# PEER gate spreading: the one-hot factors written by VectorE and ScalarE alone, in a two-block transformer kernel

## The chip, the core and the metric

The kernel runs on one core of a Trainium2 chip. The metric is the time of one execution on the device in microseconds (us). The engines are named as in the profile: PE (TensorE matmuls), PEld (its weight loads), DVE (VectorE), ACT (ScalarE), POOL (GpSimd) and SP (SyncE, which issues most DMAs). All engines run their own instruction lists in order and meet at semaphores.

## The reference, cut to what matters

Two transformer blocks run over 512 tokens of width 1024. The first block ends in a PEER layer: each token picks, in each of 8 heads, 16 experts out of 128 x 128, each with a softmax gate. Its heart is

```
v1, i1 = lax.top_k(s1, PEER_TOPK)
v2, i2 = lax.top_k(s2, PEER_TOPK)
...
e1 = jnp.take_along_axis(i1, ci // PEER_TOPK, axis=-1)
e2 = jnp.take_along_axis(i2, ci % PEER_TOPK, axis=-1)
idx = e1 * N_KEYS + e2
gates = jax.nn.softmax(sc, axis=-1).astype(h.dtype)
...
u = peer_u[ix]
a = jax.nn.gelu(jnp.einsum('td,thkd->thk', hx, u), approximate=False)
vsel = peer_v[ix]
return jnp.einsum('thk,thkd->td', gx * a, vsel)
```

The second block (Hyena, neighbourhood attention, pooling, and a mixture of 16 experts) is not touched by the change.

## The kernel before

For the last 128 of the 512 tokens the kernel gathers the chosen rows of `peer_u` and `peer_v`. For the first 384 (three tiles of 128 tokens) it computes all 16384 experts densely and weights them with a dense matrix of gates, which is zero for experts that were not chosen. That matrix is built by `spread` and is what the change touches.

A token has 128 chosen (e1, e2, gate) triples, one on each partition after a transpose: the tiles `e1T`, `e2T` and `gT` hold, per partition (one of the 128 choices) and token, the first index, the second index and the gate. The token's 128 x 128 gate matrix is then one matmul, contracted over the 128 choices, of a one-hot of e2 with a one-hot of e1 that carries the gate. `spread(t, step)` does 8 blocks of 16 tokens for each of 3 token tiles, so 24 blocks; each block has two halves (`hb`) of 8 tokens. `iob` is a constant with the values 0 to 127, each repeated 8 times. Per half:

- L572, DVE: `ob` = (iob == e1), 128 x 1024, in bf16, written densely with the 8 tokens innermost.
- L574, POOL: `of` = ob times gT, fp32, written with the token as the outer index, so that neighbouring writes lie 512 bytes apart.
- L578, DVE: `ob2` = (iob == e2), bf16, dense. In the rows it stands as `ob` or `ob_` with a number, with `e2T` as its input.
- L579, ACT: `oq` = copy of ob2 to fp32, also written with neighbours 512 bytes apart.
- L583, PE: 8 matmuls `gps` <- of, oq; the trace counts 16, since it shows each fp32 matmul as two.
- L585, ACT: two evacuations of `gps` into `st`; after both halves SP stores the block to `Gd` (L587).

After each block `step` runs two things. `early_u(1)` computes one of 40 expert groups ahead: it loads `uraw`, splits it into `uhi` (L400, ACT) and `ulo` (L401: POOL for every third group, otherwise DVE), does 24 matmuls into `aps` (L85 to L87), and ACT writes `gle` (L595). And it advances `decode`, the top-16 selection of the next token tile, mostly small DVE instructions, with four table loads and four 128 x 2048 copies (L532) on ACT in the stage.

A scheduler orders this part of the program on each engine. After it the list is written by hand (L715 on): the dense expert matmuls, paced gathers, then the second block. The pools `of`, `oq`, `ob`, `gps` and `aps` have two buffers each.

Of the kernel before, what the change touches and what calls it, by code (L numbers as in the profile page):

```python
# [9 lines left out]
F32 = mybir.dt.float32  # L10
F32R = mybir.dt.float32r
BF16 = mybir.dt.bfloat16
I32 = mybir.dt.int32
U32 = mybir.dt.uint32
AF = mybir.ActivationFunctionType
ALU = mybir.AluOpType
# [4 lines left out]
P = 128  # L21
# [343 lines left out]
def peer(px, tc, I, E):  # L365
    nc = tc.nc
    mm = nc.tensor.matmul
    act = nc.scalar.activation
    vtt = nc.vector.tensor_tensor
    vts = nc.vector.tensor_scalar  # L370
    stt = nc.vector.scalar_tensor_tensor
    ptt = nc.gpsimd.tensor_tensor
# [11 lines left out]
    e1T = kp.tile([P, TD], BF16, name="e1T", tag="e1T")  # L384
    e2T = kp.tile([P, TD], BF16, name="e2T", tag="e2T")
    gT = kp.tile([P, TD], F32, name="gT", tag="gT")
# [5 lines left out]
    EARLY = [e for e in range(P) if e % 16 in AHEAD]  # L392
    Ad = drp.tile([len(EARLY), P, TD], F32, name="Ad")

    def u_split(e, lo_engine):
        raw = up.tile([P, KD, P], F32, name="uraw", tag="uraw", bufs=4)
        nc.sync.dma_start(raw, I["peer_uT"][e])
        hi = up.tile([P, KD, P], F32R, name="uhi", tag="uhi")
        lo = up.tile([P, KD, P], F32R, name="ulo", tag="ulo")
        act(hi, raw, AF.Copy)  # L400
        lo_engine.tensor_tensor(lo, raw, hi.bitcast(F32), op=ALU.subtract)  # L401
        return hi, lo

    def u_matmuls(hi, lo):
        ps = papp.tile([P, TD], F32, name="aps", tag="aps")
        for k in range(KD):
            mm3(ps, hi[:, k], lo[:, k], hh[:, k, :TD], hl[:, k, :TD], k == 0, k == KD - 1)
        return ps

    with ExitStack() as qx:  # L410
        gp = qx.enter_context(tc.tile_pool(name="gp", bufs=2))
# [3 lines left out]
        iob = gp.tile([P, P, 8], BF16, name="iob", tag="iob", bufs=1)  # L415
# [150 lines left out]
        def spread(t, step):  # L566
            for blk in range(8 * t, 8 * t + 8):
                st = gp.tile([P, P, 16], F32, name="st", tag="st")
                for hb in range(2):
                    c0 = 16 * blk + 8 * hb  # L570
                    ob = gp.tile([P, P, 8], BF16, name="ob", tag="ob")
                    vtt(ob, iob, e1T[:, None, c0:c0 + 8].to_broadcast([P, P, 8]), op=ALU.is_equal)  # L572
                    of = gp.tile([P, 8, P], F32, name="of", tag="of")
                    ptt(of.rearrange("p t e -> p e t"), ob,  # L574
                        gT[:, None, c0:c0 + 8].to_broadcast([P, P, 8]), op=ALU.mult)
                    oq = gp.tile([P, 8, P], F32, name="oq", tag="oq")
                    ob2 = gp.tile([P, P, 8], BF16, name="ob2", tag="ob2")
                    vtt(ob2, iob, e2T[:, None, c0:c0 + 8].to_broadcast([P, P, 8]), op=ALU.is_equal)  # L578
                    act(oq.rearrange("p t e -> p e t"), ob2, AF.Copy)  # L579
                    for t4 in range(2):  # L580
                        ps = pp.tile([P, 4, P], F32, name="gps", tag="gps")
                        for j in range(4):
                            mm(ps[:, j], oq[:, 4 * t4 + j], of[:, 4 * t4 + j], start=True, stop=True)  # L583
                        o = 8 * hb + 4 * t4
                        act(st[:, :, o:o + 4], ps.rearrange("p t e -> p e t"), AF.Copy)  # L585
                for c in range(2):
                    nc.sync.dma_start(Gd[c][:, blk], st[:, 64 * c:64 * c + 64])  # L587
                step()
# [3 lines left out]
        def early_u(count):  # L592
            for n in itertools.islice(early, count):
                gl = up.tile([P, TD], F32, name="gle", tag="gle", bufs=2)
                act(gl, u_matmuls(*u_split(EARLY[n], nc.gpsimd if n % 3 == 0 else nc.vector)), AF.Gelu)  # L595
                nc.sync.dma_start(Ad[n], gl)

        for h in range(8):
# [1 line left out]
        for _ in decode(0):  # L600
            early_u(1)
        for t in range(NDT):
            dec = decode(t + 1)

            def step():
                early_u(1)
                for _ in itertools.islice(dec, 2):
                    pass

            spread(t, step)  # L610
            for _ in dec:
                pass

    early_u(len(EARLY))


# [887 lines left out]
```

## Time and profile before

| | us |
|---|---|
| median of 3 runs | 2873.01 (2872.85 to 2874.96) |
| the profiled execution | 2876.98 |
| its span, first to last instruction | 2875.2 |
| PE busy in the span | 2587.0 (90%) |
| DVE / ACT / POOL busy | 1482.8 / 941.4 / 718.8 |
| the stage of `spread` | 468.2 to about 694.5 |

The span is what the trace shows; the execution's own time is 1.8 us more. A busy share is an average over stages with different limits, so the stage of `spread` has to be read by itself.

### The profile page before, as it was taken

Reading aid. Unit: us, or ns where it says so; the run is one execution under the profiler, and the core shown is the slowest. Engines: PE = TensorE matmul, PEld = TensorE weight load, DVE = VectorE, ACT = ScalarE, POOL = GpSimd, SP = SyncE. Lnnn points to the kernel's source line nnn. Section 1 sums busy time; section 2 is a strip of 40 time slices with the busy share of each in tenths; the row PEclk is TensorE's granted clock in tenths of the full one; section 3 lists DMA queues with packets and bytes.
Section 4 is the critical chain, followed back from the end, with each engine's and each line's share of the span. In section 5 each row is a group of like instructions: output and inputs, shape, how many; then the busy total and the mean of one; then the engine's idle time right before and its main releaser. Section 6 shows DMA issues by size and latency. Waiting matters only on the chain.

```text
span 2875.2 us, 32379 instructions
## 1 busy us (share of the span) xinstructions
PE 2587.0 (90%) x12449; PEld 1806.2 (63%) x12449; DVE 1482.8 (52%) x2552; ACT 941.4 (33%) x1412; POOL 718.8 (25%) x427
## 2 busy tenths in 40 slices
PE   5798998799999999999999899969888888788887
PEld 4566888699888888888988777643322223222232
DVE  6853799984677777778878855330100101011011
ACT  5563437786333333333333434220000000000001
POOL 3411003565344444444435322110000000000000
PEclk9799999999999999999999999989999999999999
DMA  6622323467788988988889522289999999999997
GB/s 237 231 74 77 111 94 123 149 222 265 276 311 309 330 303 315 324 307 319 315 317 318 188 98 72 74 323 412 427 428 428 427 428 428 427 428 428 427 428 300
DMA packets 200451, 826.37 MB, mean 287 GB/s; under 512 B 16776, under 2 KB 85768, under 8 KB 172265
## 3 DMA queue, kind: packets, MB, share of 16 engines
q1 hardware_dynamic: 160088, 681.19, 60.4%
q0 software_dynamic: 38016, 138.43, 13.6%
q10 hardware_dynamic: 2192, 4.69, 0.5%
q8 instruction: 98, 1.61, 0.2%
q14 instruction: 57, 0.46, 0.0%
HBM read 787.02 MB, written 37.22 MB: 287 GB/s over the span
## 4 chain that ended last, share of the span: by engine, by line
PE 66%; DMA 19%; DVE 11%; ACT 2%; issue 1%; POOL 1%; ACTq 0%; SPq 0%; DVEq 0%; POOLq 0%
DMA wch<-in_w_up 10%; DMA wch<-in_w_gate 7%; PE acc L87 6%; PE acc L86 6%; PE acc L85 6%; PE aps L87 5%; PE aps L86 5%; PE aps L85 5%; PE y L1323 5%; PE upp L1298 4%; PE gp L1298 4%; PE mmp L85 4%; PE mmp L87 4%; PE mmp L86 4%; PE gps L583 2%
## 5 line engine op out<-in xcount | busy, mean ns | idle before, releaser
L1305 DVE TENSOR_TENSOR sg<-sg,upp 128x512 f32<-128x512 f32 x32 | 22.0, 688 | 752.6 <-PE upp L1298 752.6
L87 PE MATMUL aps<-hh,ulo 128*128 128x384 f32 x1024 | 347.1, 339 | 9.4 <-DVE ulo L401 6.4
L85 PE MATMUL aps<-hh,uhi 128*128 128x384 f32 x1024 | 348.5, 340 | 2.8 <-ACT uhi L400 1.8
L86 PE MATMUL aps<-hl,uhi 128*128 128x384 f32 x1024 | 347.5, 339 | 0.0
L1298 PE MATMUL upp<-wch,XB 128*64 128x512 f32 x1024 | 271.0, 627 | 51.0 <-DMA wch<-in_w_up 51.0
L85 PE MATMUL acc<-vh,wh 128*128 128x512 f32 x768 | 300.0, 391 | 1.9 <-ACT wh L81 1.9
L87 PE MATMUL acc<-vh,wl 128*128 128x512 f32 x768 | 300.7, 392 | 0.0
L86 PE MATMUL acc<-vl,wh 128*128 128x512 f32 x768 | 299.9, 390 | 0.3 <-DVE vl L82 0.3
L1298 PE MATMUL gp<-wch,XB 128*64 128x512 f32 x1024 | 263.7, 612 | 31.3 <-DMA wch<-in_w_gate 31.1
L625 POOL DMA_INDIRECT row<-in_peer_u,gidx x128 | 203.8, 1592 | 260.2 <-DVE gscr L632 228.6
L625 POOL DMA_INDIRECT row<-in_peer_v,gidx x128 | 208.1, 1626 | 238.6 <-DVE gacc L638 210.8
L1323 PE MATMUL y<-wch,aT 128*64 128x512 f32 x1024 | 246.6, 597 | 11.9 <-ACT aT L1312 11.9
L1298 PEld LDWEIGHTS upp<-wch,XB 128*64 128x64 f32 x1024 | 84.6, 144 | 215.2 <-issue 143.5
L400 ACT ACTIVATE uhi<-uraw 128x1024 fp32r<-128x1024 f32 x128 | 135.6, 1059 | 220.6 <-DMA uraw<-in_peer_uT 168.1
L1298 PEld LDWEIGHTS gp<-wch,XB 128*64 128x64 f32 x1024 | 81.3, 141 | 200.3 <-issue 149.3
L87 PEld LDWEIGHTS aps<-hh,ulo 128*128 128x128 f32 x1024 | 194.7, 190 | 12.2 <-DVE ulo L401 8.4
L85 PEld LDWEIGHTS aps<-hh,uhi 128*128 128x128 f32 x1024 | 195.1, 191 | 6.8 <-ACT uhi L400 2.0
L86 PEld LDWEIGHTS aps<-hl,uhi 128*128 128x128 f32 x1024 | 194.7, 190 | 4.0
L401 DVE TENSOR_TENSOR ulo<-uraw,uhi 128x1024 fp32r<-128x1024 f32 x114 | 149.8, 1314 | 85.1 <-ACT uhi L400 84.8
L1304 ACT ACTIVATE sg<-gp 128x512 f32<-128x512 f32 x32 | 19.1, 597 | 482.9 <-PE gp L1298 482.9
L1323 PEld LDWEIGHTS y<-wch,aT 128*64 128x64 f32 x1024 | 77.2, 137 | 150.0 <-issue 130.5
L638 DVE SCALAR_TENSOR_TENSOR gacc<-row,ga,gacc 128x1024 f32<-128x1024 f32 x128 | 164.1, 1282 | 2.3
(406 smaller groups left out, 4560.9 us busy)
## 6 DMA issues: line engine op xcount, KB each, us to landing
wch<-in_w_gate SPq DMA_DIRECT2D x64, 2048.0 KB, 32.5
wch<-in_w_up SPq DMA_DIRECT2D x64, 2048.0 KB, 32.1
wch<-in_w_down SPq DMA_DIRECT2D x62, 2048.0 KB, 33.9
uraw<-in_peer_uT SPq DMA_DIRECT2D x128, 512.0 KB, 7.7
vraw<-in_peer_v SPq DMA_DIRECT2D x128, 512.0 KB, 7.0
Gd<-st SPq DMA_DIRECT2D x48, 512.0 KB, 4.1
gg<-Gd SPq DMA_DIRECT2D x16, 1536.0 KB, 17.6
wada<-in_w_ada SPq DMA_DIRECT2D x19, 1024.0 KB, 5.2
```

What stands on the lines that cost most here:

```text
L85: mm(out, lh, rh, start=first, stop=False)
L86: mm(out, lh, rl, start=False, stop=False)
L87: mm(out, ll, rh, start=False, stop=last)
L400: act(hi, raw, AF.Copy)
L401: lo_engine.tensor_tensor(lo, raw, hi.bitcast(F32), op=ALU.subtract)
L583: mm(ps[:, j], oq[:, 4 * t4 + j], of[:, 4 * t4 + j], start=True, stop=True)
L625: nc.gpsimd.indirect_dma_start(out=row, out_offset=None, in_=I[src], in_offset=bass.IndirectOffsetOnAxis(ap=gidx[:, j:j + 1], axis=0))
L638: stt(outp, row, ga[:, n - P:n - P + 1], outp, op0=ALU.mult, op1=ALU.add)
L1298: mm(ps[64 * e:64 * e + 64], xT[:, k, 64 * e:64 * e + 64], gu[w][e][:, o:o + T], start=k == 0, stop=k == KD - 1)
L1304: act(sg, ps2[0], AF.Silu)
L1305: vtt(sg, sg, ps2[1], op=ALU.mult)
L1323: mm(y[c][64 * e:64 * e + 64], aT[:, fb, 64 * e:64 * e + 64], dn[e][:, o:o + T], start=fc == 0 and fb == 0, stop=fc == 3 and fb == 3)
```

## The change

`of` is now the bare one-hot of e1, written by DVE directly as fp32 in the layout that POOL wrote before. The gate is multiplied in on the other side: instead of one ACT copy of 1024 elements there are 8 of 128, one for each token, each of which reads every eighth element of ob2 (16 bytes apart), writes densely, and has the token's gate as its per-partition scale. The split `ulo` of `early_u` always runs on DVE. No GpSimd tensor instruction is left in this stage.

```
-                    ob = gp.tile([P, P, 8], BF16, name="ob", tag="ob")
-                    vtt(ob, iob, e1T[:, None, c0:c0 + 8].to_broadcast([P, P, 8]), op=ALU.is_equal)
                     of = gp.tile([P, 8, P], F32, name="of", tag="of")
-                    ptt(of.rearrange("p t e -> p e t"), ob,
-                        gT[:, None, c0:c0 + 8].to_broadcast([P, P, 8]), op=ALU.mult)
-                    oq = gp.tile([P, 8, P], F32, name="oq", tag="oq")
+                    vtt(of.rearrange("p t e -> p e t"), iob, e1T[:, None, c0:c0 + 8].to_broadcast([P, P, 8]),
+                        op=ALU.is_equal)
                     ob2 = gp.tile([P, P, 8], BF16, name="ob2", tag="ob2")
                     vtt(ob2, iob, e2T[:, None, c0:c0 + 8].to_broadcast([P, P, 8]), op=ALU.is_equal)
-                    act(oq.rearrange("p t e -> p e t"), ob2, AF.Copy)
+                    oq = gp.tile([P, 8, P], F32, name="oq", tag="oq")
+                    for j in range(8):
+                        act(oq[:, j], ob2[:, :, j], AF.Copy, scale=gT[:, c0 + j:c0 + j + 1])
...
-                act(gl, u_matmuls(*u_split(EARLY[n], nc.gpsimd if n % 3 == 0 else nc.vector)), AF.Gelu)
+                act(gl, u_matmuls(*u_split(EARLY[n], nc.vector)), AF.Gelu)
```

Lines behind the edit move up by one: the new L572 writes `of`, L575 writes ob2, L578 is the scaled conversion, L584 the evacuation and L594 `gle`.

On ACT, one block of the third token tile stood like this before:

```order
L400 ACTIVATE uhi<-uraw 128x1024
L595 ACTIVATE gle<-aps 128x384
L585 ACTIVATE st<-gps 128x128x4 x2
L579 ACTIVATE oq<-ob_4833 128x128x8
L585 ACTIVATE st<-gps 128x128x4 x2
L579 ACTIVATE oq<-ob_4853 128x128x8
```

and one block of the second token tile stands like this now:

```order
L578 ACTIVATE oq<-ob_4308,gT 128x128 x3
L584 ACTIVATE st<-gps 128x128x4
L578 ACTIVATE oq<-ob_4308,gT 128x128 x5
L578 ACTIVATE oq<-ob_4333,gT 128x128 x7
L594 ACTIVATE gle<-aps 128x384
L578 ACTIVATE oq<-ob_4333,gT 128x128
L584 ACTIVATE st<-gps 128x128x4
L400 ACTIVATE uhi<-uraw 128x1024
L584 ACTIVATE st<-gps 128x128x4 x2
```

Two conversions became 16, and three of the four evacuations of a block stand behind both halves' conversions.

On DVE, two blocks without decode work stood like this before:

```order
L401 TENSOR_TENSOR ulo<-uraw,uhi 128x1024
L572 TENSOR_TENSOR ob<-iob,e1T 128x1024
L578 TENSOR_TENSOR ob_4679<-iob,e2T 128x1024
L572 TENSOR_TENSOR ob<-iob,e1T 128x1024
L578 TENSOR_TENSOR ob_4699<-iob,e2T 128x1024
L572 TENSOR_TENSOR ob<-iob,e1T 128x1024
L578 TENSOR_TENSOR ob_4756<-iob,e2T 128x1024
L572 TENSOR_TENSOR ob<-iob,e1T 128x1024
L578 TENSOR_TENSOR ob_4776<-iob,e2T 128x1024
```

and one such block stands like this now:

```order
L401 TENSOR_TENSOR ulo<-uraw,uhi 128x1024
L572 TENSOR_TENSOR of<-iob,e1T 128x128x8
L575 TENSOR_TENSOR ob_4308<-iob,e2T 128x1024
L575 TENSOR_TENSOR ob_4333<-iob,e2T 128x1024
L572 TENSOR_TENSOR of<-iob,e1T 128x128x8
```

The number of one-hot instructions is the same; `of` takes the place of `ob` with another output, and `ulo` now comes once in every block.

## Rows read from the trace of the kernel before

**Rows 1.** Busy time of each engine, granted PE clock and DMA, by stretches of the stage.
```profile
core 0: us, PE busy (x) PEld busy (x) DVE busy (x) ACT busy (x) POOL busy (x), PEclk, DMA share, GB/s
468.00:500.00 32.00, 26.55 (x162) 25.67 (x162) 29.94 (x40) 22.96 (x25) 23.38 (x9) 0.88 0.39 134
530.00:560.00 30.00, 18.69 (x114) 17.38 (x114) 30.00 (x106) 20.18 (x26) 13.23 (x5) 0.89 0.37 131
...
620.00:660.00 40.00, 39.82 (x282) 38.82 (x281) 30.76 (x25) 36.55 (x42) 28.01 (x12) 1.00 0.62 221
...
468.00:695.00 227.00, 197.44 (x1331) 190.28 (x1331) 192.84 (x312) 187.12 (x207) 140.41 (x56) 0.95 0.52 186
```

**Rows 2.** Groups of instructions from 468 to 695 us: busy us, mean ns, idle before.
```profile
L572 DVE TENSOR_TENSOR ob<-iob,e1T 128x1024 bf16<-128x1024 bf16 x48 | 67.1, 1397 | 23.5 <-POOL of L574 23.5
L578 DVE TENSOR_TENSOR ob<-iob,e2T 128x1024 bf16<-128x1024 bf16 x48 | 42.9, 893 | 0.0
L401 DVE TENSOR_TENSOR ulo<-uraw,uhi 128x1024 fp32r<-128x1024 f32 x16 | 29.5, 1843 | 7.6 <-ACT uhi L400 7.6
...
L401 POOL TENSOR_TENSOR ulo<-uraw,uhi 128x1024 fp32r<-128x1024 f32 x8 | 20.9, 2617 | 10.1 <-ACT uhi L400 8.3 <-DVE ob L572 1.8
...
L547 ACT ACT_TABLE_LOAD x2 | 2.6, 1283 | 0.0
...
L532 ACT ACTIVATE wb__4573<-iif 128x2048 bf16<-128x2048 f32 x1 | 1.9, 1920 | 0.0
```

**Rows 3.** DVE in order of time: start, us, what.
```profile
639.69 2.65 DVE L572 TENSOR_TENSOR ob<-iob,e1T 128x1024 bf16<-128x1024 bf16 x1 [4.40 <-POOL of L574]
642.26 0.68 DVE L578 TENSOR_TENSOR ob<-iob,e2T 128x1024 bf16<-128x1024 bf16 x1
642.86 0.68 DVE L572 TENSOR_TENSOR ob<-iob,e1T 128x1024 bf16<-128x1024 bf16 x1
...
644.06 3.18 DVE L401 TENSOR_TENSOR ulo<-uraw,uhi 128x1024 fp32r<-128x1024 f32 x1
```

**Rows 4.** ACT in order of time, one block of the later part.
```profile
651.29 1.17 ACT L585 ACTIVATE st<-gps 128x512 f32<-128x512 f32 x2
652.36 2.02 ACT L579 ACTIVATE oq<-ob 128x1024 f32<-128x1024 bf16 x1
654.16 1.13 ACT L585 ACTIVATE st<-gps 128x512 f32<-128x512 f32 x2
655.16 2.06 ACT L579 ACTIVATE oq<-ob 128x1024 f32<-128x1024 bf16 x1
657.93 1.06 ACT L400 ACTIVATE uhi<-uraw 128x1024 fp32r<-128x1024 f32 x1 [0.70 <-PE aps L86]
658.89 0.47 ACT L595 ACTIVATE gle<-aps 128x384 f32<-128x384 f32 x1
659.26 0.59 ACT L585 ACTIVATE st<-gps 128x512 f32<-128x512 f32 x1
```

**Rows 5.** Instructions of tiles `ob` and `st`: ns min/median/max, first and last start.
```profile
L572 DVE TENSOR_TENSOR ob<-iob,e1T x48: 635/683/2675, 468.2 to 682.0; 128x1024 bf16<-128x1024 bf16 x48
...
L585 ACT ACTIVATE st<-gps x96: 573/597/672, 474.3 to 693.9; 128x512 f32<-128x512 f32 x96
```

**Rows 6.** Groups of the whole span: DVE and ACT, strided write, then dense write.
```profile
L959 DVE TENSOR_TENSOR nqkv<-mmp,rr 128x512 f32<-128x512 f32 x12 | 13.6, 1134 | 20.7 <-PE mmp L87 20.7
...
L901 DVE TENSOR_TENSOR hu<-mmp,rr 128x512 f32<-128x512 f32 x6 | 3.9, 684 | 4.9 <-ACT rr L866 4.9
...
L1003 ACT ACTIVATE nao<-op 128x512 f32<-128x512 f32 x4 | 4.3, 1081 | 2.8 <-PE op L1001 2.8
...
L289 ACT ACTIVATE ot<-op 128x512 f32<-128x512 f32 x4 | 2.4, 594 | 4.6 <-PE op L286 4.4
```

**Rows 7.** ACT in order of time: runs of eight copies with a per-partition scale.
```profile
1628.69 5.01 ACT L848 ACTIVATE hh<-X,c 128x512 fp32r<-128x512 f32 x8 [0.23 <-DVE c L845]
...
2110.70 2.17 ACT L1257 ACTIVATE XB<-pt,cols 128x128 f32<-128x128 f32 x8
```

**Rows 8.** Groups of the whole span: mean durations of ACT.
```profile
L848 ACT ACTIVATE hh<-X,c 128x512 fp32r<-128x512 f32 x8 | 5.0, 708 | 0.2 <-DVE c L845 0.2
...
L1257 ACT ACTIVATE XB<-pt,cols 128x128 f32<-128x128 f32 x64 | 17.3, 390 | 19.4 <-PE pt L1254 19.4
...
L400 ACT ACTIVATE uhi<-uraw 128x1024 fp32r<-128x1024 f32 x128 | 135.6, 1059 | 220.6 <-DMA uraw<-in_peer_uT 168.1 <-PE aps L86 34.8 <-issue 8.6
...
L133 ACT ACTIVATE sq<-X 128x512 f32<-128x512 f32 x15 | 9.3, 626 | 8.9 <-DVE X L343 8.2 <-DVE s L222 0.7
```

**Rows 9.** Waits from 695 to 740 us: who waited for whom, us in total, times, longest.
```profile
PEld aps L87 <- POOL ulo L401: 1.6, 1, 1.6
```

## The prediction

> **What bounds the kernel now.** I read the stage's windows first. The change lies wholly between 468 and 695 us [rows 1]. In its first part (468 to 560) DVE is busy all the time, 29.94 of 32 and 30.00 of 30 us, while PE gets 18.7 of 30 us of work. In its later part (620 to 660) PE is busy 39.82 of 40 us: it is the bound, and ACT comes right behind it with 36.55. So two limits follow each other, and a third engine has 9% to spare.
>
> The timeline of DVE shows why it is full. The same comparison takes 0.68 us in one place and 2.65 in another, and `ulo` 3.18 [rows 3]; the long ones lie beside a POOL tensor instruction. The group of L572 has a median of 683 ns [rows 5] and a mean of 1397 [rows 2]: of DVE's 192.8 busy us [rows 1] tens are waiting for POOL. That waiting goes with the change.
>
> The timeline of ACT gives the length of a block. From one pair of evacuations to the next it is 659.26 - 651.29 = 7.97 us [rows 4], PE's pace. ACT works 7.27 of it: 1.07 and 1.00 for the two pairs of `st`, 1.80 and 2.06 for the two conversions, 0.96 for `uhi`, 0.37 for `gle` (differences of starts, without the wait of 0.70). The stage ends with the last `st` at 693.9 + 0.6 = 694.5 us [rows 5]. Behind it come only the remaining early groups, with the same work as before, so what the stage gains or loses goes to the end nearly whole.
>
> **DVE.** Removed: 48 `ob`. Added: 48 `of` with fp32 output at a stride of 512 bytes, and 8 `ulo` that POOL did in the stage [rows 2]. The price of a strided fp32 write on DVE stands in another stage: 1134 ns for 512 elements (neighbours 32 bytes apart) against 684 for the same operation written densely [rows 6]. With about 0.15 us of fixed time, which two dense sizes give (684 ns here; an uncontended `ulo` of 1024 elements at 3.18 - 1.97, the 1.97 being the delay 2.65 - 0.68 of rows 3), that is 1.92 ns an element, so 0.15 + 1024 x 0.00192 = 2.1 us. From below: 1.2 us, if the stride cost nothing. I take 2.1. DVE then has 48 x 2.1 = 101 for `of`, 48 x 0.60 = 29 for ob2 (start to start, rows 3), about 24 x 1.15 = 28 for `ulo`, and at most 192.8 - 67.1 - 42.9 - 29.5 = 53 for decode and the rest [rows 1, 2], which still holds some of the waiting. That is 198 to 211 us where it was 193: the lock's cost is exchanged for a slower write. Without decode a block costs DVE 2 x 2.1 + 2 x 0.6 + 1.15 = 6.6 us, below PE's 7.97.
>
> **ACT.** Removed: 48 conversions, at 1.80 start to start [rows 4]. Added: 384 conversions of 128 elements with a pointer scale that read at a stride of 16 bytes and write densely. Two runs of eight scaled copies give the pace of such an instruction when it reads densely. L1257, from PSUM, 128 elements: (2.17 - 0.39) / 7 = 0.255 us [rows 7, 8]. L848, from SBUF, 512 elements: (5.01 - 0.71) / 7 = 0.615; less 384 elements at 0.84 ns, the slope between 626 ns for 512 and 1059 for 1024 [rows 8], gives 0.29. Ours read SBUF, so 0.29 is the floor that I believe, and 0.255 the lower bound.
>
> The strided read itself stands in no row. From below it costs nothing: `st` reads PSUM at a stride of 512 bytes and takes 597 ns [rows 5], a dense 512 takes 594 [rows 6]. From above it doubles the time per element, as strided SBUF writes do: L1003 takes 1081 ns against 594 [rows 6], and `oq` itself 2.02 to 2.06 us for 1024 elements against 1059 ns [rows 4, 8]. The nearest rows are those of SBUF, on both engines; they double. I take 0.84 ns more for each of 128 elements: 0.29 + 0.11 = 0.40 us. The upper bound is 0.42 (0.95 ns more, from L1003: 487 ns over 512).
>
> What the Trainium skill says of this (SBUF — State Buffer, § Specifications (TRN2)) is that SBUF has lines of 16 bytes and wants two hits in a line for full bandwidth. By that rule every read here meets a new line and pays, as in the sum below; the trace agrees for writes and has no such read.
>
> A block then costs ACT 16 x 0.40 + 1.07 + 1.00 + 0.96 + 0.37 = 9.8 us where it was 7.27, and PE needs 7.97. ACT becomes the bound.
>
> **The sum.** The first conversion can start when the first `of` and ob2 are written: 468.2 + 2.1 + 0.6 = 470.9 us. ACT has 24 x 9.8 = 235 us for the blocks, and about 14.5 for decode: four L532 at 1.9, four table loads at 1.28 [rows 2], 2 for small copies. That is 470.9 + 249.5 = 720.4. For waits I add 3.5, some 0.15 a block: three of four evacuations stand behind the conversions of both halves, with two `gps` buffers PE has to wait for them, and ACT may now and then wait back. The stage ends near 724 instead of 694.5: 29.5 later. Against that, `ulo` on DVE instead of POOL ends waits outside the stage: one of 1.6 us behind it [rows 9], and about one us in decode(0) ahead of it; I take 2.5 off. The gathers, the `gg` loads and the hand-written list behind follow at the same distance. So +27 us: the profiled execution's 2876.98 becomes 2904. It lies 4.0 above the median of its runs, so I predict **2900 us**.
>
> **The rivals.**
> - The strided read is free. Then a conversion costs 0.29 and a block 16 x 0.29 + 3.4 = 8.0 on ACT, in all 24 x 8.0 + 14.5 = 207 us, with DVE at 198 to 211 and PE at 24 x 7.97 = 191: three engines within 10% of each other, in lists that wait on each other in order. The earliest end is 468.2 + 211 = 679; with 8 to 12 us of such waits 687 to 691, or 6 us less at the end with the tail's 2.5: 2867. For it speaks `st`'s free read, against it that this is PSUM. The Trainium skill has a second wording (SBUF — State Buffer, § Door 1: The DMA port swizzle) that counts eight bf16 as the distance one may stride for free, which is exactly ours; no run here shows which holds.
> - The other side, clearly faster: also DVE's strided write is dense-priced at 1.2 us and a conversion comes at L1257's 0.255. Then DVE has 155 to 168 us, ACT 24 x 7.5 + 14.5 = 195, PE 191, and with 8 us of waits the stage ends at 470.9 + 195 + 8 = 674: 2850. It decides when a conversion costs less than about 0.31 (where 24 blocks and 14.5 us fill the time until 694.5) and `of` less than 1.7. L959 speaks against it.
> - DVE becomes the bound, because 512 bytes cost it more than the 32 of L959. From 3.2 us an `of` DVE has over 250 us, more than ACT: 2900 to 2912. Against it: ACT's writes at 256 and 512 bytes cost the same per element.
> - The moved gate changes nothing in PE's work, and the change does what it says; I give nothing to it failing in that.
>
> **How the numbers follow.** The chances: 0.68 for ACT as the bound at 0.36 to 0.42 us (2884 to 2910), 0.22 for the free read, 0.05 for the clearly faster case, 0.05 for DVE. About 0.2% (6 us) is what a measurement of this kernel can tell from no change: the free read gives half its chance to faster and half to the same; the rest follows its case. That is 0.16 faster, 0.11 the same, 0.73 slower. The likeliest case's own range is 2884 to 2912: the price of 0.42 adds 384 x 0.02 = 8 us, PSUM's fixed time (0.36) takes 15 off. The range reaches down to the middle of the free read: 2866 to 2914.
>
> **What would show it.** L578 with a pace near 0.40 us in runs of eight; L572 near 2.1 us with minimum and maximum together, no long ones; ACT busy over 95% from about 500 us on; PE below 85% in the later part; POOL idle; a block every 9.8 us; the last evacuation near 724. Wrong would make it: a conversion below 0.31 us; waits of ACT for `gps` or of PE for `oq` of more than one us a block; and PE's clock, which was granted 0.88 in the part where PE idled and 1.00 where it was full [rows 1], between its levels of 1.2 and 2.4 GHz: if PE, now idle a fifth of the time, is granted the lower one often, its 7.97 us grow toward ACT's 9.8.

## The result, and the profile after

The changed kernel takes 2910.41 us (median of 4 runs, 2907.48 to 2911.82), the kernel before beside it 2873.99 (4 runs): a ratio of 1.0124, 95% interval [1.0112, 1.0136]. It is 36 us slower; 27 were forecast. The profiled execution of after took 2907.48 us with a span of 2905.6, 30.4 us more than the span of before. It is the fastest of its runs, and that of before lay above its median, so the traces explain 30 of the 36 us.

The windows of the stage, after (to be read against [rows 1]):

```profile
core 0: us, PE busy (x) PEld busy (x) DVE busy (x) ACT busy (x) POOL busy (x), PEclk, DMA share, GB/s
468.00:500.00 32.00, 27.78 (x144) 23.41 (x144) 30.89 (x103) 31.02 (x72) 0.00 (x0) 0.85 0.38 143
...
530.00:560.00 30.00, 25.03 (x169) 23.33 (x168) 18.86 (x15) 30.00 (x68) 0.00 (x0) 1.00 0.46 157
...
590.00:620.00 30.00, 24.31 (x139) 22.13 (x138) 21.19 (x30) 29.64 (x63) 0.00 (x0) 0.89 0.41 155
620.00:660.00 40.00, 34.21 (x228) 31.70 (x226) 25.42 (x20) 40.00 (x90) 0.00 (x0) 1.00 0.48 178
```

ACT is now the engine without a gap: 30.00 of 30 us, 40.00 of 40. PE, which filled the later part, is down to 34.21 of 40, and DVE to 25.42. POOL has no instruction there.

The conversions before, from 468 to 695 us, with busy us, mean ns, and the idle time before them:

```profile
L579 ACT ACTIVATE oq<-ob 128x1024 f32<-128x1024 bf16 x48 | 98.1, 2048 | 16.0 <-DVE ob L578 16.0
```

and the groups from 460 to 735 us, after (against [rows 2]):

```profile
L578 ACT ACTIVATE oq<-ob,gT 128x128 f32<-128x128 bf16 x384 | 169.5, 540 | 3.2 <-DVE ob L575 3.2
...
L572 DVE TENSOR_TENSOR of<-iob,e1T 128x1024 f32<-128x1024 bf16 x48 | 94.3, 1989 | 10.5 <-PE gps L582 10.5
...
L401 DVE TENSOR_TENSOR ulo<-uraw,uhi 128x1024 fp32r<-128x1024 f32 x28 | 34.2, 1221 | 17.4 <-ACT uhi L400 10.4 <-DMA Gd<-st 4.1 <-PE aps L87 2.9
L575 DVE TENSOR_TENSOR ob<-iob,e2T 128x1024 bf16<-128x1024 bf16 x48 | 33.1, 689 | 49.1 <-ACT oq L578 49.1
```

The conversions were 98 us of ACT's time and are 169.5. On DVE the mean of the second comparison is 689 ns where it was 893 and that of `ulo` 1221 where it was 1843: nothing waits for POOL any more. What DVE waits for is ACT, 49.1 us in front of ob2, whose buffers ACT frees too late.

One block on ACT in order of time, after (against [rows 4]):

```profile
567.91 5.16 ACT L578 ACTIVATE oq<-ob,gT 128x128 f32<-128x128 bf16 x12
572.89 0.56 ACT L594 ACTIVATE gle<-aps 128x384 f32<-128x384 f32 x1
573.26 0.59 ACT L578 ACTIVATE oq<-ob,gT 128x128 f32<-128x128 bf16 x1
573.67 0.67 ACT L584 ACTIVATE st<-gps 128x512 f32<-128x512 f32 x1
574.14 1.14 ACT L400 ACTIVATE uhi<-uraw 128x1024 fp32r<-128x1024 f32 x1
575.09 1.15 ACT L584 ACTIVATE st<-gps 128x512 f32<-128x512 f32 x2
576.08 1.43 ACT L578 ACTIVATE oq<-ob,gT 128x128 f32<-128x128 bf16 x3
577.34 0.65 ACT L584 ACTIVATE st<-gps 128x512 f32<-128x512 f32 x1
577.82 5.17 ACT L578 ACTIVATE oq<-ob,gT 128x128 f32<-128x128 bf16 x12
```

No row has an idle time: ACT works through. From one run of twelve to the next it is 577.82 - 567.91 = 9.91 us, the block, against 7.97 before. Blocks that also hold decode work take longer, up to 13.5 us. From 464.2 to 722.1 us ACT is busy 252.3 of 257.9 us. Within the run the pace is (5.16 - 0.54) / 11 = 0.42 us a conversion (0.54 is the mean duration in the groups).

The stage's first and last instructions, after (ns min/median/max, first and last start; against [rows 5]):

```profile
L572 DVE TENSOR_TENSOR of<-iob,e1T x48: 1894/1993/2061, 464.2 to 709.7; 128x1024 f32<-128x1024 bf16 x48
...
L584 ACT ACTIVATE st<-gps x96: 570/602/671, 470.1 to 721.5; 128x512 f32<-128x512 f32 x96
```

The stage begins 4.0 us earlier (464.2 instead of 468.2) and ends at 721.5 + 0.6 = 722.1 instead of 694.5: 27.6 us later. Behind it 3 to 4 us more are lost before the first of the dense expert matmuls (`acc`), which start at 730.9 us before and at 762.2 after (ns min/median/max, first and last start; before, then after):

```profile
L85 PE MATMUL acc<-vh,wh x768: 386/390/629, 730.9 to 1618.6; 128*128 128x512 f32 x192
...
L85 PE MATMUL acc<-vh,wh x768: 389/389/628, 762.2 to 1649.6; 128*128 128x512 f32 x192
```

From there on the two run alike; 0.9 us come back by the end. SP's queue in order of time, after, shows where the time behind the stage goes:

```profile
728.04 0.54 SPq L647 DMA_DIRECT2D gg<-Gd  x1
730.81 10.45 SPq L595 DMA_DIRECT2D Ad<-gle  x1
```

and the waits from 720 to 790 us, after, show who waits for it:

```profile
ACT gle L594 <- DMA Ad<-gle: 6.9, 2, 6.6
...
PE aps L85 <- ACT gle L594: 3.9, 1, 3.9
```

The store of `gle` that follows the first big read of the gates (`gg`) holds SP for 10.45 us, so a `gle` buffer stays taken, ACT waits 6.6 us for it, and PE 3.9 for ACT. That the read is the reason is not shown. Before, the store behind the same read took 0.60 us:

```profile
699.79 0.56 SPq L648 DMA_DIRECT2D gg<-Gd  x1
...
703.35 0.60 SPq L596 DMA_DIRECT2D Ad<-gle  x1
```

### The profile page after: what moved, and what is told of

The parts are those of the page before. It is cut to its first block, busy times and chain, and to the rows that moved or that the text cites. A ratio compares the mean times of both kernels' runs of the same rounds, so it can differ in the third digit from the quotient of the medians.

```text
span 2905.6 us, 32659 instructions
## 1 busy us (share of the span) xinstructions
PE 2604.3 (90%) x12449; PEld 1816.8 (63%) x12449; DVE 1480.3 (51%) x2566; ACT 1007.4 (35%) x1748; POOL 564.6 (19%) x365
## 3 DMA queue, kind: packets, MB, share of 16 engines
q0 software_dynamic: 38016, 138.43, 13.5%
## 4 chain that ended last, share of the span: by engine, by line
PE 65%; DMA 18%; ACT 8%; DVE 7%; issue 1%; POOL 1%; DVEq 0%; SPq 0%; ACTq 0%; POOLq 0%
DMA wch<-in_w_up 10%; DMA wch<-in_w_gate 7%; PE acc L87 6%; PE acc L86 6%; PE acc L85 6%; PE aps L87 5%; PE aps L85 5%; PE aps L86 5%; PE y L1322 5%; PE upp L1297 4%; PE gp L1297 4%; PE mmp L85 4%; ACT oq L578 4%; PE mmp L86 4%; PE mmp L87 4%
## 5 line engine op out<-in xcount | busy, mean ns | idle before, releaser
L401 DVE TENSOR_TENSOR ulo<-uraw,uhi 128x1024 fp32r<-128x1024 f32 x128 | 156.4, 1222 | 79.0 <-ACT uhi L400 71.8
L578 ACT ACTIVATE oq<-ob,gT 128x128 f32<-128x128 bf16 x384 | 169.5, 540 | 3.2 <-DVE ob L575 3.2
```

The source lines that it names most:

```text
L578: act(oq[:, j], ob2[:, :, j], AF.Copy, scale=gT[:, c0 + j:c0 + j + 1])
```

## The experiments

Each run is compared with runs of the kernel before on the same chip; ratios with 95% intervals are to that kernel. The changed kernel stands at 1.0124. Only `e1_dense_read`, `e3_dense_of` and `e9_both_dense` keep the changed kernel's order of instructions on every engine in the stage. In all other runs the scheduler made a new order, so a difference of a few us there can also come from the order.

**The read made dense** (`e1_dense_read`). In the stage all engines have the same instructions in the same order as in the changed kernel.

```
-act(oq[:, j], ob2[:, :, j], AF.Copy, scale=gT[:, c0 + j:c0 + j + 1])
+act(oq[:, j], ob2.rearrange("p e t -> p (e t)")[:, j * P:(j + 1) * P], AF.Copy, scale=gT[:, c0 + j:c0 + j + 1])
```

> The changed kernel, but each conversion reads 128 neighbouring elements of ob2 instead of every eighth (so the one-hot of e2 comes out wrong; all else, and the order on every engine, is as in the changed kernel). Theory A (ACT is the bound, and the read at 16 bytes costs about 0.12 us of each conversion): start to start falls from 0.42 to 0.29 or 0.30 us, a block from 9.9 to about 8.1 us, the stage ends some 33 to 40 us earlier, the time is 2868 to 2880 us, about that of the kernel before. Theory B (the stride is free, the price is the number of instructions and their pointer scale): start to start stays at 0.42 us and the time at 2910.

2888.95 us, 1.0047 [1.0033, 1.0060]. One block on ACT in order of time, this run:

```profile
561.44 3.61 ACT L578 ACTIVATE oq<-ob,gT 128x128 f32<-128x128 bf16 x12
565.78 0.49 ACT L594 ACTIVATE gle<-aps 128x384 f32<-128x384 f32 x1 [0.72 <-PE aps L87]
```

The pace is (3.61 - 0.39) / 11 = 0.29 us: the stride costs 0.13 us of each conversion, and theory B falls. 21 us come back, but not the 30 to 42 that theory A put there: in the second token tile ACT now waits 0.72 us in a block for PE, and a block takes 8.8 us instead of 8.1. PE in turn waits for DVE's `ulo`. Two waits of this run from 468 to 700 us:

```profile
ACT gle L594 <- PE aps L87: 22.4, 13, 5.9
PEld aps L87 <- DVE ulo L401: 21.5, 15, 3.7
```

Whether DVE's slow write or the order is behind that is the question of `e9_both_dense`.

**The scale left out** (`e2_no_scale`):

```
-act(oq[:, j], ob2[:, :, j], AF.Copy, scale=gT[:, c0 + j:c0 + j + 1])
+act(oq[:, j], ob2[:, :, j], AF.Copy)
```

> The changed kernel with the gate left out: the conversions have no per-partition scale, but stay eight strided ones per half. Theory A: the pointer scale costs about 0.10 us of 0.42, so 0.32 us start to start, a block of 8.3 to 8.6 us, 2875 to 2885 us. If instead each of the 384 instructions costs a fixed time that the scale does not add to, the pace stays above 0.40 us and the time at 2905 to 2912.

2868.91 us, 0.9980 [0.9971, 0.9989]. ACT in order of time, this run:

```profile
570.74 3.12 ACT L578 ACTIVATE oq<-ob 128x128 f32<-128x128 bf16 x9
```

With the mean duration of 0.50 us that is (3.12 - 0.50) / 8 = 0.33 us a conversion. The scale costs about 0.09 us each, 384 of them 35 us; the time fell by 41.5, more than expected. The scheduler put the work of DVE, ACT and PE in another order here, so what the order gave is not separated from that. If the costs of stride and scale add up, 0.42 - 0.13 - 0.09 = 0.20 us is left for a conversion of 128 elements with neither: an estimate, not run. An eighth of an old conversion was 1.80 / 8 = 0.225 us, so by this estimate the number of instructions is not what costs.

**`of` written densely** (`e3_dense_of`); PE and ACT keep the order of the changed kernel.

```
-vtt(of.rearrange("p t e -> p e t"), iob, ...)
+vtt(of.rearrange("p t e -> p (t e)").rearrange("p (e t) -> p e t", t=8), iob, ...)
```

> The changed kernel with DVE writing of densely (the layout of the one-hot of e1 is then wrong; the order on PE and ACT is as in the changed kernel). Theory A (DVE's slower write is hidden beside ACT): L572 falls from 1.99 to about 1.2 us, DVE's busy time in the stage by some 37 us, and the time stays at 2905 to 2911 us. Theory C (the strided write on DVE sets the end): the time falls by 15 us or more, below 2896.

2905.18 us, 1.0113 [1.0097, 1.0128]: the interval overlaps that of the changed kernel. The group of this run:

```profile
L572 DVE TENSOR_TENSOR of<-iob,e1T 128x1024 f32<-128x1024 bf16 x48 | 58.6, 1222 | 12.1 <-PE gps L582 11.8
```

DVE lost 36 us of work and the medians differ by 5 us. Theory C, which asked for 15 or more, falls: beside the slow conversions DVE's slow write is hidden.

**`ulo` back on POOL** (`e4_pool_ulo`), **and off POOL in the kernel before** (`e5_before_ulo_dve`): the second edit by itself, undone and done alone.

```
-u_split(EARLY[n], nc.vector)
+u_split(EARLY[n], nc.gpsimd if n % 3 == 0 else nc.vector)
```

> The changed kernel with every third ulo on POOL again, as before. Theory A (DVE has about a quarter of the later stage to spare): DVE instructions beside those eight in the stage become about 2 us longer, and the time changes by less than 4 us, 2907 to 2914. If the moved ulo is part of the loss, the time falls by more than 5 us.

2916.18 us, 1.0141 [1.0126, 1.0157]: the median is 6 us above the changed kernel's, though the two intervals overlap, and 2 us above what theory A allowed. The time did not fall, so moving `ulo` is no part of the loss. The waits of this run from 468 to 700 us:

```profile
PE aps L87 <- POOL ulo L401: 8.5, 7, 1.9
```

> The kernel before with only the second edit: all ulo on DVE, the gate still multiplied in by POOL. By the run with ulo back on POOL (about 6 us slower than the changed kernel), this half of the change alone should give 3 to 8 us: 2867 to 2872. If it only pays where DVE has time to spare, it gives nothing here, since DVE is full in the first part: within 3 us of the kernel before.

2867.36 us, 0.9978 [0.9969, 0.9987]: in the kernel before, too, this edit alone gives 7.6 us. It pays although DVE is full there: in the stage DVE is busy 190 us with eight more splits, against 193 before, so what a split costs DVE comes back about whole as delay by POOL that is gone.

**The gate left out, one conversion of 1024 elements** (`e6_no_gate`): what it is worth that POOL is gone, when ACT does not pay.

```
-for j in range(8):
-    act(oq[:, j], ob2[:, :, j], AF.Copy, scale=gT[:, c0 + j:c0 + j + 1])
+act(oq.rearrange("p t e -> p e t"), ob2, AF.Copy)
```

> The changed kernel with the gate left out and the single conversion of 1024 elements of the kernel before on ACT: what the removal of POOL's work is worth when ACT does not pay for it. Theory A: DVE has no long instructions, a block costs ACT about 7.3 us, DVE 6.6, PE 7.9; PE bounds the later part, the stage ends 10 to 20 us earlier than in the kernel before: 2850 to 2864. Rival (DVE's slower write cancels the removed waiting): within 6 us of the kernel before.

2855.37 us, 0.9937 [0.9924, 0.9951]: 19.6 us faster than before. The gain that the change aimed at exists (the move of `ulo`, 7.6 us when done alone, is part of it), and it is lost again on ACT: 2910.4 - 2855.4 = 55 us for putting the gate there in this form.

**Both one-hots of a token by DVE** (`e7_dve_scalars`). `iob` is a row of 128 numbers, e1T and e2T are kept in fp32; no ob2, no conversion. The new lines:

```
+for j in range(8):
+    c = c0 + j
+    vts(of[:, j], iob, e1T[:, c:c + 1], None, op0=ALU.is_equal)
+    vts(oq[:, j], iob, e2T[:, c:c + 1], gT[:, c:c + 1], op0=ALU.is_equal, op1=ALU.mult)
```

> Both one-hots on DVE, one instruction of 128 elements for a token each, dense: compare the row of 128 numbers with the token's index as a per-partition scalar, and for the second multiply by the gate in the same instruction; no conversion on ACT, no ob2. If such an instruction takes about 0.14 us start to start on DVE, a block costs DVE 32 x 0.14 + 1.15 = 5.6, ACT 3.4 and PE 7.9 us: PE bounds the stage, 2840 to 2856. If it takes 0.22 us or more, DVE needs 8.2 us a block and 40 to 50 for decode: 2885 or more.

2888.70 us, 1.0050 [1.0037, 1.0064]. DVE in order of time, this run:

```profile
560.25 0.28 DVE L575 TENSOR_SCALAR of<-iob,e1T 128x128 f32<-128x128 bf16 x1
560.45 0.34 DVE L576 TENSOR_SCALAR oq<-iob,e2T,gT 128x128 f32<-128x128 bf16 x1
560.71 0.28 DVE L575 TENSOR_SCALAR of<-iob,e1T 128x128 f32<-128x128 bf16 x1
```

0.20 us for the one and 0.26 for the other, start to start, not 0.14: DVE is busy 192.00 of 192 us from 468 to 660 and bounds the stage. ACT's work can't simply be given to DVE.

**Numbers innermost everywhere** (`e8_token_outer`): the constant and both one-hots are laid out token by token, so that nothing strides.

```
-vtt(of.rearrange("p t e -> p e t"), iob, e1T[:, None, c0:c0 + 8].to_broadcast([P, P, 8]), op=ALU.is_equal)
+vtt(of, iob, e1T[:, c0:c0 + 8, None].to_broadcast([P, 8, P]), op=ALU.is_equal)
...
-act(oq[:, j], ob2[:, :, j], AF.Copy, scale=gT[:, c0 + j:c0 + j + 1])
+act(oq[:, j], ob2[:, j], AF.Copy, scale=gT[:, c0 + j:c0 + j + 1])
```

> The changed kernel with the numbers innermost in the constant and in both one-hots, so that every write and read is dense and the result is the reference's. Theory A: conversions at 0.29 us as in the run with the dense read, and of at 1.2 us; ob2 stays at 0.69 or goes to 1.2 us, both hidden. The time is that of the dense read or a little less: 2878 to 2890.

2869.11 us, 0.9977 [0.9968, 0.9986]: 41 us less than the changed kernel and 6 less than before, and better than expected: the forecast came from `e1_dense_read`, and the next run shows what held that one. ob2 went from 0.69 to 1.22 us, `of` from 1.99 to 1.22. The group of ob2, this run:

```profile
L574 DVE TENSOR_TENSOR ob<-iob,e2T 128x1024 bf16<-128x1024 bf16 x48 | 58.6, 1221 | 25.1 <-ACT oq L577 25.1
```

**Both dense in the changed kernel's order** (`e9_both_dense`): the edits of `e1_dense_read` and `e3_dense_of` together.

> The two dense forms together in the changed kernel: conversions read 128 neighbouring elements and DVE writes of densely (both one-hots then have a wrong layout); the order on PE, ACT and SP is as in the changed kernel. If the 2889 us of the dense read alone were held by DVE's slower write (DVE full in the first part, of 0.8 us longer in each half), this gives 10 to 20 us more: 2869 to 2879, as with the token-outer layout. If they were held by the order alone, which was made for slower conversions, it stays at 2884 to 2890.

2869.61 us, 0.9978 [0.9969, 0.9987]. So it was DVE's slower write that held `e1_dense_read`, not the order: the same write that costs about 5 us beside the slow conversions costs 19 beside the fast ones. DVE need not be full for that: in the stage of `e1_dense_read` it is busy 185 of 237.5 us, and full only at the start (32.00 of 32 us from 468 to 500). Elsewhere `ulo` comes late from DVE, and PE waits for it. With the dense write this wait is down to a third (468 to 690 us):

```profile
PEld aps L87 <- DVE ulo L401: 7.1, 6, 2.1
```

A hidden cost shows as soon as its cover is gone.

**A split of the scaled one-hots of e2 between DVE and ACT** (`e10_six_two`, `e11_seven_one`, `e12_five_three`), all on `e8_token_outer`, with e2T in fp32 and ob2 only as long as ACT needs it; the main lines of the first:

```
+for j in range(6, 8):
+    c = c0 + j
+    vts(oq[:, j], iob[:, 0], e2T[:, c:c + 1], gT[:, c:c + 1], op0=ALU.is_equal, op1=ALU.mult)
+for j in range(6):
+    act(oq[:, j], ob2[:, j], AF.Copy, scale=gT[:, c0 + j:c0 + j + 1])
```

> The token-outer kernel with two of each eight scaled one-hots of e2 written by DVE in one instruction (compare with the index, times the gate) and six converted by ACT as there. By the measured paces, ACT goes from about 209 to 181 us in the stage, DVE from 178 to about 189, PE stays at 191: if ACT bounds the token-outer kernel, 4 to 15 us less than it, 2855 to 2866; if waits in order hold it, within 3 us of 2869.

> The same with one of eight on DVE: ACT 195, DVE about 184, PE 191 us. Half of the gain of the run with two of eight, 2860 to 2867; more than there if DVE is what holds that one.

> Token-outer with three of each eight one-hots of e2 on DVE and five converted by ACT. In the run with two of eight PE was busy 189 of 192 us, DVE 183, ACT 178. One more takes 14 us from ACT and adds about 48 x (0.255 - 0.14) = 6 us to DVE, which is not the engine with time to spare: 2840 to 2850, no faster than 2842.

| on DVE, of 8 | us | ratio to before |
|---|---|---|
| 0 (`e8_token_outer`) | 2869.11 | 0.9977 [0.9968, 0.9986] |
| 1 (`e11_seven_one`) | 2850.30 | 0.9917 [0.9903, 0.9930] |
| 2 (`e10_six_two`) | 2842.00 | 0.9887 [0.9872, 0.9902] |
| 3 (`e12_five_three`) | 2845.66 | 0.9903 [0.9887, 0.9920] |

Windows of `e10_six_two`:

```profile
468.00:660.00 192.00, 189.45 (x1333) 184.84 (x1332) 183.00 (x411) 178.15 (x442) 0.00 (x0) 1.00 0.62 223
```

and of `e12_five_three`:

```profile
468.00:660.00 192.00, 187.56 (x1316) 181.92 (x1315) 186.37 (x456) 165.24 (x393) 0.00 (x0) 1.00 0.58 215
```

With two, PE is busy 189 of 192 us and DVE and ACT are close behind. With three, ACT has time to spare and DVE has more to do; the two times can't be told apart for certain. The runs with one and with two beat their forecasts by 10 and 13 us: `e10_six_two` gains 27 us on `e8_token_outer`, where 4 to 15 were expected, 33 on the kernel before and 68 on the changed one. Why so much is open. The order is new, and PE's granted clock differs: the stage's work kept PE busy 205 us at a mean clock of 0.96 in `e8_token_outer` and 188 us at 1.00 in `e10_six_two`, whose stage takes 190.8 us. PE, with 24 blocks of 7.95 us, is its bound.

## Why the prediction was right, step by step

- **ACT becomes the bound.** Right, and shown from two sides: `e1_dense_read` and `e2_no_scale` shorten ACT's conversions and the time falls by 21 and 41.5 us; `e3_dense_of` and `e4_pool_ulo` change DVE and POOL and gain 5 us at most.
- **The conversion at 0.40 us.** Measured 0.42, the upper bound. The doubling of the time per element was the right choice between the two ends: without the stride it is 0.29, as the run of L848 gave [rows 7]. The scale's share, about 0.09 us by `e2_no_scale`, was inside that row. For ACT's reads of SBUF 16 bytes from element to element are not free. The prediction named two wordings of the Trainium skill (SBUF — State Buffer, § Specifications (TRN2) and § Door 1: The DMA port swizzle): a line of 16 bytes wants two hits, and one may stride over eight bf16 for free. The trace agrees with the first and not with the second (0.42 us against 0.29). That lines are the reason is not shown, since no run tried another step.
- **The block at 9.8 us.** Measured 9.91. 24 x 9.91 = 238 us. With 14.5 us for decode that is 252.5, and ACT was busy 252.3. In such a block all four evacuations, not three, stand behind the conversions of both halves. Still the 3.5 us for waits were about right: ACT was idle 5.6 us of the stage's 257.9, 2.6 of them before its first conversion.
- **The end of the stage at 724.** 722.1. Two errors cancel, which is luck: the conversion's pace was 5% higher (some 3 us over 24 blocks), and the first conversion came at 466.8 instead of 470.9, because the stage began 4.0 us earlier. Of these, 2.4 us were there before the first token tile's selection, decode(0), began (its first `VVs` comes at 320.2 us instead of 322.6), where both kernels do the same work; `e1_dense_read`, with the same order up to there, has 323.4. Only the other 1.6 fall in decode(0), which the prediction put at about one.
- **`of` at 2.1 us on DVE.** 1.99, minimum and maximum within 0.17 us of each other: the price of a 32-byte stride carried over to 512 bytes. DVE's total of 198 to 211 us was too high: it is busy 188 us in the stage. The 53 us for decode and the rest held more waiting for POOL than was allowed for: the group of L543 went from 17.2 to 7.3 us and that of L544 from 7.3 to 1.7.
- **The 2.5 us off for the tail.** This step failed. The wait for POOL's `ulo` behind the stage is gone, but a store that SP could not finish for 10.45 us brought a new wait of 3.9 us on PE. The end of the stage is 27.6 us later and the first `acc` 31.3 us. SP's order there is nearly that of before, where ACT waited 2.2 us for such stores and PE not at all; why the store takes so long at this moment was not tested. It is no accident of this one trace: in the traces of all twelve experiments PE waits there for `gle`, 1.3 to 5.5 us in all. The part of the term behind the stage was -1.5 and measured about +3.7. That is most of what lies between the 27 us forecast and the 30 of the traces; the other 6 us, up to 36, are the spread of the runs.
- **PE's clock.** It was granted 0.85 to 0.95 in stretches with decode work and 1.00 from 530 to 590 and from 620 to 660 us, although PE idled a sixth of those. Over the stage the mean is 0.95, as before. With ACT as the bound it did not become a term.
- **The rival with the free read, at 2867.** `e1_dense_read` is this case with the rest of the change kept, and takes 2889. The rival's price was wrong by 22 us. It let the stage end at 687 to 691 us, with DVE the longest engine at up to 211 us and 8 to 12 us of waits on top. It ends at 704.9, and DVE is busy only 185 us of it, so the waits were mis-sized. In `e9_both_dense`, without the strided write, it ends at 687.5, and the time is 2870. The change would have lost even with a free read.

## What to carry to other kernels

Before work is moved off an engine that blocks another, price it on the engine that receives it, instruction by instruction from rows of the same memory and operand kind: here what was taken off POOL was worth 20 us and its replacement cost 55. Strided access was paid here on both sides, by ACT's reads at 16 bytes and by DVE's writes at 512; when a constant can be laid out so that all accesses are dense, as in `e8_token_outer`, do that first. Then divide the rest by measured paces until the engines are equally full: the best kernel here keeps three of them above 92% from 468 to 660 us.

## What the runs showed that was not expected

- A comparison in bf16 whose second input repeats its innermost element takes longer: 1.22 us for 1024 elements against 0.69 with eight distinct neighbours (`e8_token_outer` against the changed kernel).
- A DVE comparison of 128 elements with a per-partition index takes 0.20 us start to start, with a second per-partition factor 0.26; a TENSOR_SCALAR of 128 fp32 elements with constants (L513 in decode) takes 0.14.
- One store of 192 KB held SP's queue for 10.45 us behind a read of 1.5 MB, where such a store took 0.60 us in the kernel before; through ACT, PE waited 3.9 us for it. The cause is open.
